# Background modulation chunks as VectorE rows, and merge adds on GpSimd, in a two-layer hybrid backbone

## The chip, the cores and the metric

The kernel is one program on one core of a Trainium2 chip. The metric is the device time of one execution in microseconds. It was 1999.94 us, the median of three runs (1998.57 to 2007.31).

## The reference

Two layers work on 256 context and 256 latent tokens of width 1024. Each layer has two sub-layers, and each is modulated by the conditioning vectors `c` (latent) and `c_ctx` (context). The modulation is six vectors ("chunks") of 1024 a layer, for both streams:

```python
mod_x = jnp.split((sc @ ada_w[l] + ada_b[l])[:, None, :], ADA_CHUNKS, axis=-1)    # sc = silu(c)
mod_c = jnp.split((scc @ ada_w[l] + ada_b[l])[None, None, :], ADA_CHUNKS, axis=-1)
hx = modulate(xx, norm1_g[l], mod_x[0], mod_x[1])          # the same for the context
mc, mx = token_mixer(hc, hx, p, lower[l], row, col, lam_init, last)
xx = xx + mod_x[2] * mx
hx = modulate(xx, norm2_g[l], mod_x[3], mod_x[4])
xx = xx + mod_x[5] * expert_choice_moe(hx, ...)
```

The token mixer has four branches (GLA scan, Hyena convolution, HGRN2 scan, differential attention). They are merged by gates and projected out:

```python
gates = jax.nn.sigmoid(gate_cols.reshape(B, L, N_BRANCH, D_MODEL))
merged = gates[:, :, 0] * (outs[0] @ w_branch[0])
for i in range(1, N_BRANCH):
    merged = merged + gates[:, :, i] * (outs[i] @ w_branch[i])
return merged @ w_out
```

Differential attention is softmax(q1 k1) - lam softmax(q2 k2) times v, per head and in blocks of 128 queries. The expert layer lets each of 16 experts take its best 32 tokens.

## The kernel before, in words

Activations are kept as columns: a tile has 128 channels on its partitions and 512 tokens along it. A scheduler sets the order of every engine's instructions when the program is built, and each engine then works off its own queue in that fixed order.

**The modulation in the first layer's mixer.** Chunks (layer, chunk) come about in two ways. `AdaBack` makes them on TensorE in the background: `Ada.step` (L465ff) loads a tile of 512 KB of `ada_w` (L469) into one of two buffers and makes four matmuls into a tile `pa`; eight such tiles are a chunk, and `mod_write` (L446) transposes the result into place. `run` (called in `load`, L842ff, with 2 credits a column block, and with half a credit at each scan level) decides when. Chunks (0,2), (0,3), (0,4) are done so: 24 tiles. `AdaRows` makes the others on VectorE, with the transposed weights `ada_t`: one tile is 128 outputs, and two instructions (L527), one for each stream, multiply it by the conditioning vector and sum along the row. The vector comes in as `cb`, spread over the partitions (L507), and goes through Silu on ScalarE (L508). Two buffers of 512 KB are loaded ahead (L515). Chunks (0,5), (1,1), (1,0) are done so: 24 tiles.

**The merges.** `merge(br, first)` (L892) goes through 8 blocks of 128 output channels. For each it loads a gate column block (L842), splits it into a high part on ScalarE (L843) and a low part on VectorE (L844), makes 24 matmuls into `pd`, takes tanh on ScalarE (L897), makes six matmuls of the branch into `pa` (its weights are split at L719, every fourth block), multiplies on VectorE (L905), and adds to the accumulator on VectorE (L911; not in the first merge). After L905, `rows.step` does one row tile in merges 0, 2 and 3 (`br != 1`): 24 blocks, 24 tiles.

**The order of the mixer.** The Hyena filters (L722 to L775) run early beside the first column blocks; then the two scans; then differential attention (from L1196), whose 32 score products are reduced on VectorE (L1250), go through exp on ScalarE (L1252), are normalised on VectorE (L1255 to L1257) and transposed on TensorE (`pm`, L428). The scheduler fills the scans and attention with merges 0 and 2. Then come hyena (L1318 to L1384), merges 3 and 1 and the out-projection (L1421), and after it the experts, whose weights come in at the full rate of the loads. GpSimd's queue also issues two loads for hyena (L1315, L1316).

Of the kernel before, what the change touches and what calls it, by code (L numbers as in the profile page):

```python
# [14 lines left out]
OP = mybir.AluOpType  # L15
# [4 lines left out]
KB = 8  # L20
# [9 lines left out]
FL = (1, 1)  # L30
DAS = (0.5, 1)
ADA = (2, 2)
ROWS = ((0, 5), (1, 1), (1, 0))
FIRST = ("gk", "gq")
AHEAD = ((0, 0), (0, 5))

# [317 lines left out]
def build(tc, ins, outT, dbg=None, stop=None):  # L354
    nc = tc.nc
    V, A, T, G, S = nc.vector, nc.scalar, nc.tensor, nc.gpsimd, nc.sync
    big = tc.tile_pool(name="big", bufs=1)
    pool = big.__enter__()
    mem = Mem(pool.tile([128, BASE], F32, name="base"), BASE, small=768)
# [140 lines left out]
    class AdaRows:  # L500


        def __init__(self, keep):
            self.todo = [(i, j) for i in range(len(ROWS)) for j in range(KB)]
            self.raw, self.junk, self.cb = [mem.take(1024, keep) for _ in range(2)], mem.take(1024, keep), mem.take(2048, keep)
            src = ins["cb"]
            S.dma_start(out=self.cb(n=2048), in_=bass.AP(tensor=src.tensor, offset=src.offset, ap=[[0, 128], [1, 2048]]))  # L507
            A.activation(self.cb(n=2048), self.cb(n=2048), AF.Silu)  # L508
            self.n = self.at = 0
            self.load(), self.load()  # L510
# [6 lines left out]

        def step(self, after):

            if self.n == len(self.todo):  # L520
                return
            i, j = self.todo[self.n]
            l, c = ROWS[i]
            b = self.raw[self.n % 2]
            with tc.issue_after(after.ins):
                for s in range(2):
                    V.tensor_tensor_reduce(self.junk() if s == 0 else b(), b(), self.cb(s * 1024, n=1024), 1.0,  # L527
                                           cs("adab", l * 48 + c * 8 + j, n=1), OP.mult, OP.add,
                                           mod[l](c * 16 + j * 2 + s, n=1))
            self.n += 1  # L530
            self.load()
            if self.n == len(self.todo):
                for b in self.raw + [self.junk, self.cb]:
                    b.free()
# [249 lines left out]
    def mixer(l, last, ada_bg, rm, sums):  # L784
# [18 lines left out]
        for k in range(KB):  # L803
# [3 lines left out]
            for s in range(2):  # L807
                c = slice(s * 256, s * 256 + 256)
# [83 lines left out]
        def merge(br, first):  # L892
            o = ob[br]
            for d in range(KB):
                p = col_block(f"m{br}{d}", t0)
                g = view(accb, d * W, W) if first and l else mem.take(W, keep_x if first else None)
                A.activation(g(), p, AF.Tanh, scale=0.5)  # L897
                if d % 4 == 0:
                    load_wb(br, d // 4)
                p = ps("s" if ada_bg.left else "a")  # L900
                for fb in range(2):
                    w = [b(((d % 4) * 2 + fb) * 128, n=128) for b in wbs]
                    mm3(p[:, 0:W], w, (o(2 * fb * W, n=W), o((2 * fb + 1) * W, n=W)),
                        fb == 0, fb == 1)
                gated = V.scalar_tensor_tensor(g(), g(), 1.0, p[:, 0:W], op0=OP.add, op1=OP.mult)  # L905
                if l == 0 and br != 1:
                    rows.step(gated)
                if first:
                    acc[d] = g
                else:  # L910
                    V.tensor_tensor(acc[d](), acc[d](), g(), op=OP.add)  # L911
                    g.free()
            o.free()

# [866 lines left out]
    for l in range(2):  # L1781
        with phase("right", F32R) as rm:
            if l == 0:
                ada = AdaBack([(0, c) for c in range(2, 5)], mem.take(2048))
            pre, ahead = mixer(l, l == 1, ada, rm, sums)
        if stop == "mixer0":
            dump("mod0", mod[0]())
# [27 lines left out]
```

## Time and profile before

| | us |
|---|---|
| median of three runs | 1999.94 (1998.57 to 2007.31) |
| the profiled execution, its own time | 2006.5 |
| its span in the profile | 2004.7 |
| TensorE (PE) busy | 1843.2 |
| VectorE (DVE) busy | 854.7 |
| ScalarE (ACT) busy | 529.9 |
| GpSimd (POOL) busy | 27.9 |

The profile is of one execution. PEld is TensorE's weight load, SP the engine that issues most loads, and SPq a queue's own part. "PEclk" or the granted clock is the share of full speed that TensorE was given: 1.00 is 2.4 GHz, 0.50 is 1.2 GHz. A name such as `pd<-r` means output and input tiles, "<-DMA base<-ada_w" the thing that ended a wait. One matmul of the program can be two records in the trace. Times on the time line are from the span's beginning.

### The profile page before, as it was taken

The page shows a single profiled execution, that of the slowest core. Times are in us where ns is not written, and L with a number is a line of the kernel's source. Part 1 is how long each engine was busy: PE and PEld are TensorE (multiplying, and loading weights), DVE is VectorE, ACT ScalarE, POOL GpSimd, SP SyncE. Part 2 cuts the span into 40 slices and gives each one's busy share as a digit, 9 for nine tenths or more (in the row PEclk, how much of TensorE's full clock was granted, in tenths as well). Part 3 has the DMA queues.
Part 4 walks back from the last instruction along what each step waited for, and adds up shares of the span by engine and source line. Part 5 has one row for each costly group of instructions (what it writes and reads, how often), then busy time and mean ns, then how long its engine had stood idle before and what let it go on. Part 6 is the DMA issues. An engine that isn't in the chain of part 4 may idle for free.

```text
span 2004.7 us, 28151 instructions
## 1 busy us (share of the span) xinstructions
PE 1843.2 (92%) x11524; PEld 1087.6 (54%) x11524; DVE 854.7 (43%) x1855; ACT 529.9 (26%) x932; POOL 27.9 (1%) x52
## 2 busy tenths in 40 slices
PE   7999999999999899999897799999998999987877
PEld 3667778877887443434232356788997333221213
DVE  5355658798743222221121345869865021110101
ACT  4433447522233110101000243447443000000000
POOL 0000000000000000000000010010000000000000
PEclk9989999999999899999999999999998999999999
DMA  8641122364545999999999855333578999999999
GB/s 312 223 140 58 64 85 78 107 236 136 194 156 218 353 399 350 387 409 409 409 409 409 302 189 180 117 106 137 200 262 336 409 409 409 409 409 409 409 409 332
DMA packets 154148, 550.07 MB, mean 274 GB/s; under 512 B 11042, under 2 KB 22690, under 8 KB 153124
## 3 DMA queue, kind: packets, MB, share of 16 engines
q1 hardware_dynamic: 153444, 545.13, 71.7%
q0 software_dynamic: 576, 3.15, 0.5%
q8 instruction: 91, 1.49, 0.3%
q14 instruction: 37, 0.30, 0.0%
HBM read 545.08 MB, written 3.15 MB: 273 GB/s over the span
## 4 chain that ended last, share of the span: by engine, by line
PE 69%; DMA 19%; DVE 7%; issue 3%; ACT 3%; SPq 0%; DVEq 0%; ACTq 0%
PE pd L431 40%; PE ps L431 15%; DMA base<-moe_w 8%; PE pm L431 7%; DMA r<-moe_w 6%; PE pa L431 4%; DMA base<-ada_w 2%; PE pm L428 1%; DMA base<-wg 1%; DVE base L527 1%; DVE r L844 1%; ACT r L843 1%; PE ps L1640 1%; DMA base<-cb 0%; DVE r L1236 0%
## 5 line engine op out<-in xcount | busy, mean ns | idle before, releaser
L431 PE MATMUL pd<-r 128*128 128x256 f32 (+3 forms) x2976 | 574.4, 364 | 12.9 <-DMA r<-moe_w 6.5
L431 PEld LDWEIGHTS pd<-r 128*128 128x128 f32 (+2 forms) x2976 | 427.3, 184 | 131.4 <-issue 53.8
L431 PE MATMUL pd<-r,r 128*128 128x512 f32 (+3 forms) x1304 | 282.6, 433 | 13.4 <-DMA r<-moe_w 10.8
L431 PEld LDWEIGHTS pd<-r,r 128*128 128x128 f32 (+2 forms) x1304 | 161.8, 166 | 105.0 <-issue 54.8
L844 DVE TENSOR_TENSOR r<-base,r 128x1024 fp32r<-128x1024 f32 x136 | 165.9, 1222 | 110.4 <-ACT r L843 110.0
L843 ACT ACTIVATE r<-base 128x1024 fp32r<-128x1024 f32 x136 | 143.4, 1058 | 252.2 <-PE pd L431 181.2
L431 PE MATMUL ps<-base 32*64 32x64 f32 (+12 forms) x2372 | 177.2, 279 | 15.1 <-DMA base<-hy 5.1
L431 PE MATMUL pd<-r,base 128*32 128x512 f32 (+1 forms) x680 | 166.5, 598 | 11.3 <-DMA r<-moe_w 10.6
L431 PEld LDWEIGHTS ps<-base 32*64 32x64 f32 (+7 forms) x2372 | 112.6, 142 | 76.3 <-issue 42.7
L431 PE MATMUL pm<-base 128*128 128x128 f32 (+12 forms) x660 | 106.1, 327 | 17.5 <-DVE base L1571 5.8
L431 PE MATMUL ps<-r,base 128*64 128x512 f32 (+4 forms) x468 | 98.6, 525 | 12.9 <-DVE base L1641 6.3
L431 PE MATMUL pd<-base 128*32 128x512 f32 (+1 forms) x408 | 100.5, 595 | 6.4 <-DMA base<-moe_w 5.6
L431 PEld LDWEIGHTS pm<-base 128*128 128x128 f32 (+5 forms) x660 | 72.8, 180 | 60.9 <-issue 33.6
L431 PEld LDWEIGHTS pd<-r,base 128*32 128x32 f32 (+1 forms) x680 | 42.0, 122 | 111.2 <-issue 76.4
L1637 DVE TENSOR_TENSOR r<-base,pd 64x512 f32<-64x512 f32 x16 | 10.9, 679 | 214.3 <-PE pd L431 214.3
L1637 DVE TENSOR_TENSOR base<-base,pd 128x512 f32<-128x512 f32 x16 | 11.0, 688 | 190.1 <-PE pd L431 155.9
L1636 ACT ACTIVATE base<-pd 128x512 f32<-128x512 f32 (+1 forms) x32 | 19.0, 594 | 251.1 <-PE pd L431 251.1
L431 PE MATMUL pa<-r,r 128*128 128x512 f32 (+1 forms) x384 | 82.4, 342 | 1.1 <-DVE base L905 1.1
L1687 ACT ACTIVATE base<-ps 32x512 f32<-32x512 f32 (+2 forms) x28 | 14.7, 525 | 251.6 <-PE ps L431 247.2
L1687 ACT ACTIVATE r<-ps 32x512 f32<-32x512 f32 (+2 forms) x32 | 15.3, 480 | 246.2 <-PE ps L431 240.3
L431 PE MATMUL pd<-base,r 128*32 128x512 f32 (+1 forms) x296 | 71.3, 597 | 9.3 <-DMA base<-moe_w 9.3
L1685 DVE COPY r<-ps 32x512 f32<-32x512 f32 (+2 forms) x32 | 17.8, 555 | 123.3 <-ACT r L1687 123.2
(246 smaller groups left out, 1728.8 us busy)
## 6 DMA issues: line engine op xcount, KB each, us to landing
r<-moe_w SPq DMA_DIRECT2D x251, 1024.0 KB, 18.1
base<-moe_w SPq DMA_DIRECT2D x131, 1024.0 KB, 17.4
base<-wg SPq DMA_DIRECT2D x152, 512.0 KB, 3.6
base<-ada_w SPq DMA_DIRECT2D x60, 512.0 KB, 4.7
base<-ada_t SPq DMA_DIRECT2D x24, 512.0 KB, 3.3
r<-ada_w SPq DMA_DIRECT2D x12, 512.0 KB, 10.2
base<-xT SPq DMA_DIRECT2D x4, 1024.0 KB, 6.8
filters<-r SPq DMA_DIRECT2D x8, 256.0 KB, 4.0
```

What stands on the lines that cost most here:

```text
L428: T.transpose(out, in_, ident)
L431: return T.matmul(out, lhsT, rhs, start=start, stop=stop, **kw)
L527: V.tensor_tensor_reduce(self.junk() if s == 0 else b(), b(), self.cb(s * 1024, n=1024), 1.0, cs("adab", l * 48 + c * 8 + j, n=1), OP.mult ...
L843: A.activation(w[0](), raw(), AF.Copy)
L844: V.tensor_tensor(w[1](), raw(), F(w[0]()), op=OP.subtract)
L1636: A.activation(s_(np_=rows), pa[0:rows, :], AF.Silu)
L1637: V.tensor_tensor(h_(np_=rows), s_(np_=rows), pb[0:rows, :], op=OP.mult)
L1640: T.transpose(p[:, q * rows:q * rows + rows], h_(q * 128, n=128, np_=rows), cs("ident", n=rows, np_=rows))
L1685: V.tensor_copy(dst, src)
L1687: A.activation(dst, src, AF.Copy)
```

## The change

Four lines do it. The row chunks become (0,4), (0,3), (0,2), (0,5), (1,1): 40 tiles in place of 24. The background on TensorE keeps one chunk, (1,0): 8 tiles in place of 24. `step` is now called in all 32 merge blocks of the first layer and does 1.25 tiles a block on the average. And the adds of merges 2 and 3 in the first layer go to GpSimd; those of merge 1 stay on VectorE. From L517 on the lines of the changed kernel are 3 higher: its row instruction is L530, its gated product L908, its add L914, its attention reduction L1253.

```diff
-ROWS = ((0, 5), (1, 1), (1, 0))
+ROWS = ((0, 4), (0, 3), (0, 2), (0, 5), (1, 1))
...
-            self.todo = [(i, j) for i in range(len(ROWS)) for j in range(KB)]
+            self.todo, self.due = [(i, j) for i in range(len(ROWS)) for j in range(KB)], 0
...
         def step(self, after):
 
-            if self.n == len(self.todo):
-                return
+            self.due += len(self.todo) / (4 * KB)
+            while self.n < self.due:
+                self.tile(after)
+
+        def tile(self, after):
             i, j = self.todo[self.n]
...
                 gated = V.scalar_tensor_tensor(g(), g(), 1.0, p[:, 0:W], op0=OP.add, op1=OP.mult)
-                if l == 0 and br != 1:
+                if l == 0:
                     rows.step(gated)
                 if first:
                     acc[d] = g
                 else:
-                    V.tensor_tensor(acc[d](), acc[d](), g(), op=OP.add)
+                    (V if l or br == 1 else G).tensor_tensor(acc[d](), acc[d](), g(), op=OP.add)
                     g.free()
...
-                ada = AdaBack([(0, c) for c in range(2, 5)], mem.take(2048))
+                ada = AdaBack([(1, 0)], mem.take(2048))
```

The scheduler's order moves with it. TensorE's queue in the filter stretch, as a difference (`pa_762` is a background chunk, `ps` the filters, `pd` a column block):

```order
 L431 MATMUL ps_604<-base 64x256
-L431 MATMUL pa_762<-base 32x256 x8
-L431 MATMUL pd_1153<-r_227,r_231 128x512 x13
-L431 MATMUL pa_762<-base 32x256 x4
-L431 MATMUL pd_1153<-r_227,r_231 128x512 x8
+L431 MATMUL pd_1122<-r_227,r_231 128x512 x24
+L431 MATMUL pd_1152<-r_227 128x512 x4
 L431 MATMUL ps_614<-r_530,base 64x256
-L431 MATMUL pa_762<-base 32x256 x4
-L431 MATMUL pd_1153<-r_227,r_231 128x512 x3
-L431 MATMUL pd_1199<-r_227 128x512
-L431 MATMUL pa_762<-base 32x256 x4
```

The background tiles that stood between the column block's matmuls are gone, and the matmuls of the next block have moved up into their place.

TensorE's queue in the second half of attention, before (`ps` from `r_678` are score products, `pm` transposes, `ps` from `base` products with v, `pd` and `pa` the merges):

```order
L431 MATMUL pd_3198<-r_227 128x512 x3
L431 MATMUL ps_2723<-base 128x64 x2
L431 MATMUL pd_3198<-r_227 128x512
L431 MATMUL pa_3224<-r_678,r_231 128x512
L431 MATMUL ps_2802<-r_678 128x512
L431 MATMUL pa_3224<-r_678,r_231 128x512 x5
L431 MATMUL pd_3238<-r_227,r_231 128x512
L431 MATMUL ps_2832<-r_678 128x256
L431 MATMUL pd_3238<-r_227,r_231 128x512 x2
L428 MATMUL pm_2787<-base 128x128 x4
L431 MATMUL pd_3238<-r_227,r_231 128x512 x3
L431 MATMUL ps_2837<-r_678 128x256
```

The same piece of attention in the changed kernel (its tile numbers are 94 lower: `ps_2708` was `ps_2802`):

```order
L431 MATMUL pd_3150<-r_227,r_231 128x512 x2
L431 MATMUL ps_2629<-base 128x64 x2
L431 MATMUL ps_2703<-r_678 128x512
L431 MATMUL pa_3096<-r_678,r_231 128x512 x5
L431 MATMUL ps_2708<-r_678 128x512
L431 MATMUL pa_3096<-r_678,r_231 128x512
L431 MATMUL ps_2738<-r_678 128x256
L428 MATMUL pm_2693<-base 128x128 x4
L431 MATMUL ps_2743<-r_678 128x256
L431 MATMUL ps_2629<-base 128x64 x4
L431 MATMUL ps_2757<-r_678 128x256
L431 MATMUL ps_2762<-r_678 128x256
```

Between these score products there were column blocks' matmuls (`pd`); now `pd` is left out but for two, and the first blocks after attention have them.

VectorE's queue at the same place before (L1250 reduces a score product, L1257 normalises):

```order
L1250 TENSOR_REDUCE base<-ps_2802 128x1
L1257 SCALAR_TENSOR_TENSOR base<-base 128x512
L1251 TENSOR_SCALAR base<-base 128x1
L1236 CAST r_678<-r_678 32x512
L1250 TENSOR_REDUCE base<-ps_2832 128x1
L844 TENSOR_TENSOR r_227<-base,r_227 128x1024
L1255 RECIPROCAL base<-base 128x2
L1251 TENSOR_SCALAR base<-base 128x1
L1250 TENSOR_REDUCE base<-ps_2837 128x1
L1256 SCALAR_TENSOR_TENSOR base<-base 128x1
L1251 TENSOR_SCALAR base<-base 128x1
L905 SCALAR_TENSOR_TENSOR base<-base,pa_3224 128x512
```

And in the changed kernel (L530 is the row instruction and its read-out):

```order
L1253 TENSOR_REDUCE base<-ps_2708 128x1
L1260 SCALAR_TENSOR_TENSOR base<-base 128x512
L1254 TENSOR_SCALAR base<-base 128x1
L1239 CAST r_678<-r_678 32x512
L1253 TENSOR_REDUCE base<-ps_2738 128x1
L530 ISA base<-base 128x1024
L530 ISA base 128x1
L1258 RECIPROCAL base<-base 128x2
L1254 TENSOR_SCALAR base<-base 128x1
L1253 TENSOR_REDUCE base<-ps_2743 128x1
L1259 SCALAR_TENSOR_TENSOR base<-base 128x1
L1254 TENSOR_SCALAR base<-base 128x1
```

The low-part split L844 and the gated product L905 have gone from between the softmax steps, and row instructions stand there. In all 16 of them stand before the last attention product L1260, five in its first half, where before all stood behind it.

## Rows read from the trace of the kernel before

**Rows 1.** The page: busy time by engine; then the chain that ended last.

```profile
PE 1843.2 (92%) x11524; PEld 1087.6 (54%) x11524; DVE 854.7 (43%) x1855; ACT 529.9 (26%) x932; POOL 27.9 (1%) x52
...
PE 69%; DMA 19%; DVE 7%; issue 3%; ACT 3%; SPq 0%; DVEq 0%; ACTq 0%
```

**Rows 2.** Stretches: us, busy us (count) of PE, PEld, DVE, ACT, POOL; PEclk, DMA share, GB/s.

```profile
400.00:450.00 50.00, 48.11 (x203) 38.81 (x202) 49.24 (x76) 12.06 (x15) 0.54 (x1) 0.97 0.68 235
...
550.00:600.00 50.00, 50.00 (x219) 40.53 (x218) 23.60 (x31) 16.93 (x23) 0.00 (x0) 1.00 0.44 155
```

**Rows 3.** TensorE: its waits for `ada_w` from 60 to 300 us; one background tile.

```profile
PE pa L431 <- DMA base<-ada_w: 4.4, 6, 1.4
...
104.03 0.64 PE L431 MATMUL pa<-base 128*32 128x256 f32 x8 [1.25 <-DMA base<-ada_w]
104.60 0.74 PE L431 MATMUL pd<-r 128*128 128x512 f32 x2
```

**Rows 4.** Chain of work from 80 to 115 us, shares by line.

```profile
by line: DMA base<-ada_w 45.9%; PE pd L431 22.5%; PE ps L431 22.5%; PE pa L431 7.5%; PE ps L428 2.4%; issue 0.5%
```

**Rows 5.** Slices of 4 us of the same stretch, columns as in rows 2.

```profile
96.00:100.00 4.00, 2.71 (x16) 1.69 (x17) 0.38 (x2) 0.42 (x1) 0.00 (x0) 1.00 0.56 186
...
104.00:108.00 4.00, 3.97 (x26) 3.37 (x27) 0.38 (x2) 1.06 (x1) 0.00 (x0) 0.73 0.71 227
108.00:112.00 4.00, 4.00 (x13) 3.22 (x12) 1.80 (x4) 0.00 (x0) 0.00 (x0) 0.50 0.01 5
```

**Rows 6.** The attention stretch, columns as in rows 2.

```profile
303.30:377.30 74.00, 73.89 (x396) 59.71 (x395) 63.24 (x179) 52.11 (x118) 0.00 (x0) 1.00 0.23 79
```

**Rows 7.** Attention stretch: TensorE's merge matmuls, VectorE's lines that the order moves.

```profile
L431 PE MATMUL pd<-r 128*128 128x512 f32 x113 | 30.5, 401 | 0.0
L431 PE MATMUL pd<-r,r 128*128 128x512 f32 x61 | 18.3, 408 | 0.0
L431 PE MATMUL pa<-r,r 128*128 128x512 f32 x42 | 12.4, 402 | 0.0
...
L1250 DVE TENSOR_REDUCE base<-ps 128x1 f32<-128x512 f32 x16 | 11.0, 687 | 3.8 <-PE ps L431 3.8
L844 DVE TENSOR_TENSOR r<-base,r 128x1024 fp32r<-128x1024 f32 x8 | 9.7, 1222 | 2.3 <-ACT r L843 2.3
```

**Rows 8.** VectorE in order of time: start us, us, engine line op.

```profile
395.91 1.28 DVE L527 CUSTOM_DVE_ANT_0 base<-base 128x1024 f32<-128x1024 f32 x1
...
397.11 0.68 DVE L905 SCALAR_TENSOR_TENSOR base<-base,pa 128x512 f32<-128x512 f32 x1
397.71 1.28 DVE L527 CUSTOM_DVE_ANT_0 base<-base 128x1024 f32<-128x1024 f32 x1
```

**Rows 9.** TensorE in a later merge block: start us, us, engine line op.

```profile
560.16 5.66 PE L431 MATMUL pd<-r 128*128 128x512 f32 x24
565.66 1.55 PE L431 MATMUL pa<-r,r 128*128 128x512 f32 x6
```

**Rows 10.** ScalarE's table load for Silu of `cb`, and VectorE's first row instruction.

```profile
390.13 1.28 ACT L508 ACT_TABLE_LOAD   x1 [1.23 <-DMA base<-cb]
...
393.37 1.29 DVE L527 CUSTOM_DVE_ANT_0 base<-base 128x1024 f32<-128x1024 f32 x1 [2.29 <-ACT base L508]
```

**Rows 11.** TensorE at hyena's beginning.

```profile
443.62 7.33 PE L431 MATMUL pd<-r 128*128 128x512 f32 x24 [1.89 <-DVE base L1328]
```

**Rows 12.** GpSimd's groups; GpSimd's casts in the second layer, and VectorE beside them.

```profile
L817 POOL TENSOR_TENSOR r<-base,r 128x256 fp32r<-128x256 f32 x3 | 2.2, 730 | 0.2
...
1349.37 3.57 POOL L1236 CAST r<-r 32x512 fp32r<-32x512 f32 x4
...
1348.87 0.41 DVE L1198 TENSOR_TENSOR base<-base 128x256 f32<-128x256 f32 x1
...
1349.94 0.83 DVE L1199 TENSOR_TENSOR base<-base 128x256 f32<-128x256 f32 x1
```

**Rows 13.** Chain in the MoE's routing: start, us, what.

```profile
650.28 1.28 ACT L1454
```

## The prediction

> **What bounds the kernel now.** Read the engines' busy time first: TensorE works 92% of the span, VectorE 43% [rows 1]. The chain of the work that ended last is TensorE's for 69% of the span, with single links of VectorE and of loads [rows 1]. Then the stretches of the first mixer: from 400 to 450 us TensorE has 48.1 of 50 us of work and VectorE 49.2, from 550 to 600 us 50.0 and 23.6 [rows 2]. So TensorE is the bound there, and VectorE in places the next one. For the change two stretches count more than these averages. In the filter stretch, 60 to 106 us, TensorE waits for the background tiles' weights [rows 3, 4]. In the attention stretch, 303 to 377 us, TensorE is busy 73.89 of 74.00 us only because merge matmuls fill the gaps of the softmax, while VectorE is busy 63.24 [rows 6].
>
> The sum is made against the profiled execution, 2006.5 us (span 2004.7). The median of the three runs is 1999.94, so I apply the difference to the median. About 0.5%, 10 us, is what a measurement can tell from no change.
>
> **Term A, what TensorE loses in work: -14.5 us.** 16 of the 24 background tiles leave TensorE; the first 8 stay and stand where they stood. One tile is 8 records, and the next matmul starts 0.57 us after it (104.03 to 104.60) [rows 3]: 16 x 0.57 = 9.1 us. TensorE waits 4.4 us for their weights in six pieces, all but one small one of which belong to tiles that go: 4.1 us [rows 3]. Where it waits, TensorE is busy 2.7 of 4 us, and the granted clock falls from 1.00 to 0.73 and then 0.50 in slices of full work: 4 x (0.27 + 0.50) = 3.1 us [rows 5]. Together 16.3. The filter branch's own matmuls then wait on their VectorE steps with less to fill in; I take 1.8 back. Bounds: -10 (the work alone) and -21.6, if the chain's links to these loads, 45.9% of its 35 us or 16.1 us [rows 4], all go and the nine tiles after 106 us add about 5.5.
>
> **Term B, attention: +24.1 us.** The 32 added VectorE instructions for sixteen tiles do not only replace TensorE's; the static order moves. Before, the copy of `cb` was issued after attention, and the first row instruction ran at 393.37 us, behind its Silu [rows 10]. In the changed order the first stands inside attention, and 16 row instructions (8 tiles) come before its last product. One takes 1.20 us with its read-out (395.91 to 397.11), a gated product 0.60 [rows 8]. VectorE's sum there: 63.2 + 16 x 1.20 (19.2), less what the order takes out: 4 low-part splits of 1.22 us that overlap their neighbour by 0.08 (4.6), 2 gated products (1.2) and one split of branch weights of the same shape as L844 (1.1) [rows 7, 8]. That is 75.5 us, against 74.
>
> TensorE's share shrinks at once. Before, 113 + 61 + 42 = 216 merge matmuls lie in the stretch [rows 7], at 0.23 us each (5.50 us for 24, from 560.16 to 565.66) [rows 9]: 49.9 us, which leaves 24.0 of 73.9 to attention itself. The changed order has 158 there: 128 up to the middle, and 30 in the second half, half of those behind the last scores. First half, to the sixteenth of 32 score products: TensorE 128 x 0.23 + 12.0 = 41.4 us, VectorE 63.2 / 2 + 5 x 1.20 = 37.6; TensorE sets it. Second half: TensorE 30 x 0.23 + 12.0 = 18.9 us, VectorE 31.6 + 11 x 1.20 - 6.9 = 37.9; VectorE sets it. So 79.3 us, of which TensorE works 60.3: it idles 19.0. I add 2 for VectorE's own waits on score matmuls (3.8 us in the stretch now, half of it [rows 7]) and 3.1 for one fall of the clock as in the filter stretch [rows 5], since TensorE would be busy only half of the second half. Bounds: 15, VectorE's bare 75.5 less 60.3; and 33, if VectorE also keeps today's idle 74.0 - 63.2 = 10.8 us [rows 6]: 19.0 + 3.1 + 10.8. Silu and its table load come between two exponentials on ScalarE: 3.24 us from 390.13 to 393.37, and 1.28 for the table back [rows 10], in the first half, where VectorE has 4 us of slack; nothing, at most +4.5 without that slack, inside the 33.
>
> **Term C, entry to hyena: -3.5 us.** After attention VectorE now works off its queue of row tiles, and TensorE waits 1.89 us for L1328 at 443.62; the next 24 matmuls take 7.33 us, against 5.66 elsewhere, at a lower clock [rows 11, 9]. 1.89 + 1.67 = 3.5. The changed order has no row instruction among hyena's steps. Bounds 0 and -5.
>
> **The small terms.** A merge block costs VectorE 1.14 + 0.28 (a quarter of a branch split) + 0.60 + 2.5 x 1.20 = 5.0 us, in merge 1 5.6 with its add, against 30 x 0.23 = 6.9 on TensorE [rows 7 to 9]: the 24 tiles of the later blocks cost nothing, and cover ends where a block's VectorE work passes 6.9. At the end of merge 1 the last block's tile, 2 x 1.20, stands ahead of the last add: +0.5 (0 to 2.4). A table load of 1.28 us in the chain at 650.28 [rows 13] is not in the changed ScalarE order: -1.3. Loads: 16 tiles of 512 KB change their source, not their size; SP's early copy of `cb` falls in a stretch with a DMA share of 0.23 [rows 6]: 0. On POOL's queue the load of the filters now stands behind one add of some 1.5 us, and hyena, which reads it, comes eight blocks later: 0.
>
> **The adds on GpSimd: 0.** Sixteen adds of 0.60 leave VectorE. On GpSimd the nearest row is a 256-wide tensor_tensor of 0.73 us [rows 12], so about 1.46 for 512. Nobody is close behind: the accumulator is next read one merge later. But it is not free for VectorE: while GpSimd runs four casts for 3.57 us, a 256-wide VectorE add takes 0.83 us beside one of 0.41 [rows 12]. If each add costs VectorE as much as it saves, nothing is won; bounds 0 and +8 (below).
> The Trainium skill, "SBUF — State Buffer", section "Who interferes with whom", speaks against this edit: VectorE instructions with two SBUF inputs, which the row instructions and splits are, and GpSimd instructions that read SBUF exclude each other for a whole instruction. The trace agrees in kind, by the doubled add; it shows no GpSimd add of this width.
>
> **Sum.** -14.5 + 24.1 - 3.5 + 0.5 - 1.3 + 0 = **+5.3 us** on 1999.94: **2005**. No change that a measurement can tell, with the sign leaning to slower.
>
> **The rivals.**
> 1. *Faster, 1989 us.* The filter branch is freed wholly and attention costs only VectorE's bare work: -21.6 + 15 - 4.3 = -10.9. For it: those links to loads are in the chain [rows 4]. Against it: TensorE itself waits only 4.4 us there [rows 3], and the first half of attention is long for TensorE, so that VectorE cannot run without a gap. 0.17.
> 2. *Slower, 2019 us.* VectorE becomes the bound of attention's second half with its present waits, at TensorE's 1.2 GHz level: -10 + 33 - 4 = +19. It decides where TensorE's idle time in attention passes 26 us, 5 more than the forecast's 21, since then the sum passes 10. For it: with 18.9 us of work in 38 TensorE would be less busy than before the fall in rows 5, and each softmax group goes from TensorE to VectorE, ScalarE and back. Against it: the row instructions themselves fill VectorE's waits. 0.27.
> 3. *Adds that block, 2014 us.* Each add holds VectorE for 1.46: a block becomes 6.5 us, 7.4 with the add's wait behind two row instructions, against 6.9; 16 x 0.5 = 8 more. It decides where VectorE in a merge block has no gap left. Against it: VectorE is busy 23.6 of 50 us in the later blocks now [rows 2]. 0.08.
> 4. *The forecast, 2005.* 0.48.
> The skill's exclusion of those two engines, named above, is rival 3's mechanism; by it VectorE would lose 1.46 us an add.
>
> **How the numbers follow.** Range 1989 to 2020: rival 1's time to just above rival 2's. Within the forecast's case the bounds of A and B put 0.1 on faster by over 0.5% and 0.27 on slower. Faster: 0.17 x 0.6 + 0.48 x 0.1 + little = 0.17. Slower: 0.27 x 0.85 + 0.48 x 0.27 + 0.08 x 0.6 = 0.41, less a little since rival 2's gaps may be filled: 0.38. Same: 0.45.
>
> **What would show it.** A: no `ada_w` wait on TensorE after about 90 us, and the attention stretch beginning near 289 us instead of 303.3 [rows 6]. B: from the first L1253 reduction to the last product about 80 us, TensorE's idle time in it near 20 us with VectorE as releaser, in the second half, and a granted clock below 0.9 there. C: no wait for hyena's VectorE step. GpSimd: 16 adds of about 1.5 us; VectorE's row instructions still 1.28. I am wrong if TensorE stays above 95% busy through attention, if the filter stretch gains under 8 us, or if the merge blocks after hyena take more than 7 us each.

## The result, and the profile after

The changed kernel takes 2023.55 us (median of 4 runs, 2021.68 to 2024.86), the kernel before 2001.47 beside it (4 runs). The ratio is **1.0101, 95% interval 1.0075 to 1.0126**: about 20 us slower. The forecast was 2005 with a range up to 2020. The time lies behind its upper end, and on the slower side, which had 0.38.

The profiled execution of the changed kernel has a span of 2022.7 us, 18.0 longer than that of before. Its page, busy time and chain of work, against [rows 1]:

```profile
PE 1849.0 (91%) x11392; PEld 1096.6 (54%) x11392; DVE 894.4 (44%) x1897; ACT 531.7 (26%) x932; POOL 61.3 (3%) x68
...
PE 69%; DMA 19%; DVE 6%; issue 3%; ACT 3%; SPq 0%; DVEq 0%; ACTq 0%
```

The shares are the same to a per cent, and the page alone doesn't say where the time went. Marks along the way do. The table has the first attention reduction, hyena's first step (L1328, or what became of it) and the out-projection's first result (L1421), all VectorE's, in the profiled executions:

| | before | changed | difference |
|---|---|---|---|
| to the first attention reduction | 303.7 | 294.6 | -9.1 |
| from there to hyena's first step | 139.0 | 165.1 | +26.1 |
| from there to the out-projection | 158.5 | 159.7 | +1.2 |
| from there to the end of the span | 1403.5 | 1403.3 | -0.2 |

So between these two executions the filter stretch gave 9.1 us, the way through attention cost 26.1, and what follows changed little: the experts' stage passes the shift on. The stretches of 50 us, columns as in rows 2:

```profile
300.00:350.00 50.00, 42.23 (x203) 33.16 (x201) 41.45 (x107) 35.02 (x69) 0.00 (x0) 0.88 0.24 85
350.00:400.00 50.00, 43.72 (x179) 33.96 (x180) 43.69 (x108) 21.26 (x47) 0.69 (x1) 0.74 0.37 126
400.00:450.00 50.00, 50.00 (x219) 40.73 (x218) 42.80 (x54) 12.31 (x16) 14.44 (x8) 1.00 0.62 211
...
550.00:600.00 50.00, 50.00 (x219) 40.72 (x218) 44.31 (x64) 12.96 (x16) 4.41 (x2) 1.00 0.58 193
```

From 400 us on TensorE is full; before, it had 48.1 of 50 us of work from 400 to 450 [rows 2]. From 300 to 400 us it is busy 86 of 100 us where it was full, and its granted clock is 0.88 and 0.74. Slices of attention show it closer (the 74 us of before were one row [rows 6]):

```profile
294.00:334.00 40.00, 38.90 (x194) 30.79 (x193) 33.41 (x91) 28.53 (x56) 0.00 (x0) 1.00 0.25 92
334.00:344.00 10.00, 6.87 (x34) 5.68 (x32) 8.18 (x22) 9.05 (x19) 0.00 (x0) 0.72 0.00 1
344.00:354.00 10.00, 6.46 (x20) 4.51 (x19) 9.28 (x30) 2.04 (x6) 0.00 (x0) 0.50 0.46 156
354.00:364.00 10.00, 7.26 (x22) 5.02 (x21) 8.47 (x23) 6.29 (x14) 0.00 (x0) 0.59 0.17 55
364.00:374.00 10.00, 7.72 (x31) 5.90 (x31) 7.88 (x25) 3.89 (x12) 0.00 (x0) 0.58 0.33 105
374.00:384.00 10.00, 8.79 (x37) 7.00 (x38) 9.44 (x21) 3.62 (x10) 0.00 (x0) 0.73 0.19 61
384.00:394.00 10.00, 9.94 (x52) 8.13 (x51) 8.31 (x21) 3.40 (x6) 0.69 (x1) 1.00 0.71 254
```

The first half is whole. From 334 us, where the order has almost no merge matmul left, TensorE is busy 6.5 to 8.8 of 10 us, and those at a granted clock of 0.50 to 0.73. Between 294 and 394 us it idles 14.1 us, and the clock takes busy time x (1 - clock) = 1.9 + 3.2 + 3.0 + 3.2 + 2.4 = 13.7 us more from 334 to 384. That is 27.8 in all, an account of TensorE's time and not of causes. Merge matmuls from the first reduction to the sixteenth score product and from there to the last product are 124 and 25 records in the trace, before 101 and 109. TensorE's longest waits from 280 to 700 us that the change brought:

```profile
PE ps L431 <- ACT base L1264: 5.5, 6, 2.3
PE pa L431 <- DVE base L908: 3.4, 1, 3.4
```

L1264 is the eviction of the transposed probabilities on ScalarE: a step of the softmax chain, which TensorE now stands and waits for. The row instructions are there as the order said, behind Silu:

```profile
311.79 1.28 ACT L508 ACT_TABLE_LOAD   x1 [2.27 <-DMA base<-cb]
313.09 1.91 ACT L508 ACTIVATE base<-base 128x2048 f32<-128x2048 f32 x1
...
315.03 1.28 DVE L530 CUSTOM_DVE_ANT_0 base<-base 128x1024 f32<-128x1024 f32 x1 [3.33 <-ACT base L508]
```

The filter stretch of the changed kernel in slices of 4 us, against [rows 5]:

```profile
100.00:104.00 4.00, 2.37 (x12) 1.99 (x11) 2.17 (x4) 2.22 (x4) 0.00 (x0) 0.86 0.38 131
104.00:108.00 4.00, 4.00 (x16) 3.51 (x16) 0.61 (x2) 0.00 (x0) 0.00 (x0) 0.50 0.00 0
...
116.00:120.00 4.00, 4.00 (x115) 3.12 (x113) 2.41 (x4) 2.95 (x8) 0.00 (x0) 0.99 0.38 137
120.00:124.00 4.00, 3.90 (x27) 3.08 (x23) 3.74 (x8) 1.21 (x2) 0.00 (x0) 0.50 0.00 0
124.00:128.00 4.00, 4.00 (x68) 3.23 (x67) 2.23 (x6) 0.62 (x1) 0.00 (x0) 0.50 0.02 6
...
136.00:140.00 4.00, 4.00 (x55) 3.78 (x57) 2.37 (x7) 0.63 (x1) 0.00 (x0) 0.50 0.24 94
140.00:144.00 4.00, 4.00 (x39) 3.78 (x35) 3.52 (x8) 0.00 (x0) 0.00 (x0) 0.52 0.02 4
```

After the first fall, which is there before as well [rows 5], the clock falls twice more: 0.50 from 120 to 128 us and 0.50 and 0.52 from 136 to 144, in slices where TensorE is full. It was full in the slice ahead of 120 too, so idle time in these slices doesn't explain the fall. The stretch from 120 to 148 us before, then changed:

```profile
120.00:148.00 28.00, 27.18 (x500) 19.77 (x497) 22.70 (x47) 9.59 (x19) 2.17 (x4) 0.94 0.35 109
```

```profile
120.00:148.00 28.00, 27.23 (x398) 23.36 (x396) 21.13 (x46) 6.64 (x12) 2.44 (x4) 0.64 0.07 21
```

The wait for `ada_w` is gone, as forecast [rows 3], and the filters' and scans' steps are what TensorE waits for:

```profile
PE ps L431 <- DVE base L987: 2.2, 4, 0.8
...
PE pa L431 <- DMA base<-ada_w: 0.3, 1, 0.3
```

Two of GpSimd's adds, then VectorE's lines of the same moment, in order of time (start us, us):

```profile
404.16 2.21 POOL L914 TENSOR_TENSOR base<-base 128x512 f32<-128x512 f32 x1 [16.61 <-DVE base L908]
...
413.02 1.28 POOL L914 TENSOR_TENSOR base<-base 128x512 f32<-128x512 f32 x1 [5.75 <-DVE base L908]
...
403.93 1.28 DVE L530 CUSTOM_DVE_ANT_0 base<-base 128x1024 f32<-128x1024 f32 x1
...
405.17 2.28 DVE L847 TENSOR_TENSOR r<-base,r 128x1024 fp32r<-128x1024 f32 x1
...
411.11 1.22 DVE L847 TENSOR_TENSOR r<-base,r 128x1024 fp32r<-128x1024 f32 x1
```

Over all 16 adds and all 80 row instructions (min/median/max in ns):

```profile
L914 POOL TENSOR_TENSOR base<-base x16: 1282/2203/2271, 404.2 to 557.3; 128x512 f32<-128x512 f32 x16
...
L530 DVE CUSTOM_DVE_ANT_0 base<-base x80: 1264/1278/2401, 315.0 to 613.7; 128x1024 f32<-128x1024 f32 x80
```

An add alone takes 1.28 us. Where it meets a row instruction that has begun, it takes 2.2, and the split that comes next on VectorE takes 2.28 in place of 1.22: by these times one waits for the other and then the other for the one. The row instruction at 403.93, which was first, keeps its 1.28; seven of the 80 take 2.2 to 2.4. The Trainium skill, "SBUF — State Buffer", section "Who interferes with whom", says that a VectorE instruction with two inputs in SBUF contends with a GpSimd instruction that reads SBUF, by an exclusive lock; the trace agrees for this pair, with these numbers. It cost little here: TensorE is full from 400 us on, and e1 below, without these adds, can't be told from the changed kernel.

### The profile page after: what moved, and what is told of

The parts are those of the page before. It is cut to its first block, busy times and chain, and to the rows that moved or that the text cites. A ratio compares the mean times of both kernels' runs of the same rounds, so it can differ in the third digit from the quotient of the medians.

```text
span 2022.7 us, 27972 instructions
## 1 busy us (share of the span) xinstructions
PE 1849.0 (91%) x11392; PEld 1096.6 (54%) x11392; DVE 894.4 (44%) x1897; ACT 531.7 (26%) x932; POOL 61.3 (3%) x68
## 4 chain that ended last, share of the span: by engine, by line
PE 69%; DMA 19%; DVE 6%; issue 3%; ACT 3%; SPq 0%; DVEq 0%; ACTq 0%
PE pd L431 40%; PE ps L431 15%; DMA base<-moe_w 9%; PE pm L431 6%; DMA r<-moe_w 6%; PE pa L431 5%; DMA base<-wg 2%; DMA base<-ada_w 1%; PE pm L428 1%; DVE r L847 1%; ACT r L846 1%; PE ps L1643 1%; DVE r L1239 0%; DMA base<-cb 0%; ACT r L1237 0%
## 5 line engine op out<-in xcount | busy, mean ns | idle before, releaser
L431 PE MATMUL pd<-r,r 128*128 128x512 f32 (+3 forms) x1304 | 280.1, 433 | 13.7 <-DMA r<-moe_w 10.9
L431 PE MATMUL ps<-base 32*64 32x64 f32 (+12 forms) x2372 | 181.7, 286 | 19.1 <-ACT base L1264 5.8
L431 PEld LDWEIGHTS ps<-base 32*64 32x64 f32 (+7 forms) x2372 | 118.3, 151 | 77.7 <-issue 38.5
L431 PE MATMUL pm<-base 128*128 128x128 f32 (+12 forms) x660 | 105.5, 325 | 17.6 <-DVE base L1574 5.8
L530 DVE CUSTOM_DVE_ANT_0 base<-base 128x1024 f32<-128x1024 f32 x80 | 108.8, 1364 | 5.7 <-ACT base L508 3.3
```

Source lines behind the costliest of these rows:

```text
L431: return T.matmul(out, lhsT, rhs, start=start, stop=stop, **kw)
```

## The experiments

All ratios are to the kernel before on the same chip in the same job. It lay between 1996 and 2020 us there, so the ratios count, not the medians. Marks as in the table above, each from one profiled execution: they tell where the time goes, the ratios how much. The part behind the out-projection, where no edit changes the code, took 1402 to 1411 us in them.

| run | row tiles: number, merges | first reduction | to hyena | to out-projection | ratio, interval |
|---|---|---|---|---|---|
| before | 24 in 0, 2, 3 | 303.7 | 139.0 | 158.5 | 1 |
| changed | 40 in all | 294.6 | 165.1 | 159.7 | 1.0101 (1.0075 to 1.0126) |
| e1 | 40 in all, adds VectorE | 295.3 | 162.4 | 159.7 | 1.0091 (1.0065 to 1.0116) |
| e2 | before, adds GpSimd | 297.5 | 143.3 | 160.3 | 1.0021 (0.9999 to 1.0042) |
| e3 | 40 in 2, 3, 1 | 295.5 | 142.8 | 170.2 | 1.0036 (1.0015 to 1.0057) |
| e5 | 24 in 2, 3, 1, two chunks out | 296.0 | 136.4 | 159.8 | 0.9969 (0.9949 to 0.9990) |
| e6 | e3, adds VectorE | 295.8 | 141.8 | 167.9 | 1.0043 (1.0027 to 1.0059) |
| e7 | 32 in 2, 3, 1 | 293.6 | 137.9 | 159.5 | 1.0014 (0.9984 to 1.0044) |
| e8 | before, 24 in 2, 3, 1 | 297.0 | 135.4 | 159.7 | 0.9994 (0.9970 to 1.0018) |
| e9 | e5 with fill | 293.2 | 135.4 | 159.7 | 0.9947 (0.9931 to 0.9963) |
| e10 | changed, buffer held | 303.6 | 143.6 | 167.6 | 1.0074 (1.0054 to 1.0095) |
| e11 | changed with fill | 294.5 | 145.2 | 173.8 | 1.0033 (1.0012 to 1.0053) |
| e12 | changed, scores thrice | 295.4 | 167.7 | 159.7 | 1.0104 (1.0068 to 1.0141) |
| e13 | e11, adds VectorE | 292.2 | 142.1 | 173.8 | 1.0025 (1.0008 to 1.0041) |
| e14 | e8, four buffers | 303.0 | 144.7 | 158.9 | 1.0046 (1.0025 to 1.0068) |
| e15 | e7, four buffers | 307.7 | 142.9 | 159.5 | 1.0047 (1.0023 to 1.0071) |
| e16 | e5, 24 in 0, 2, 3 | 293.9 | 152.8 | 158.4 | 1.0045 (1.0023 to 1.0066) |
| e18 | e7 again | 294.0 | 137.8 | 159.6 | 0.9990 (0.9964 to 1.0016) |
| e17 | e7 with fill | 299.5 | 135.5 | 160.7 | 0.9956 (0.9939 to 0.9972) |

**Are the adds the loss? e1 and e2.** The first theory after the result was that attention makes the loss; the rival was GpSimd.

```diff
-                    (V if l or br == 1 else G).tensor_tensor(acc[d](), acc[d](), g(), op=OP.add)
+                    V.tensor_tensor(acc[d](), acc[d](), g(), op=OP.add)
```

> The changed kernel with all merge adds back on VectorE. Theory (the loss is made in attention, where row instructions stand in place of merge matmuls; the adds on GpSimd are free): 2021 to 2026 us, TensorE idle about 14 us between 294 and 394 us as in the changed kernel. Rival (the 2.2 us adds on GpSimd and the VectorE instructions they double are what costs): 2012 us or less.

> The kernel before with only the adds of merges 2 and 3 moved to GpSimd. Theory (adds free): within 4 us of the kernel before, about 2001; single VectorE instructions of over 2 us beside an add, and TensorE still without a wait there. Rival (adds cost): 2010 us or more.

e1 stays at 1.0091: the rival is out for the changed kernel. e2 stands at 1.0021 and its interval touches no change. It isn't quite free: there VectorE works off its row tiles at hyena's beginning, the doubled instructions lengthen that, and TensorE's wait of 1.89 us [rows 11] becomes

```profile
PE pd L431 <- DVE base L1328: 4.8, 1, 4.8
```

**Is it row tiles inside attention? e3 and e16.** e3 takes them out of merge 0, the one that the order lays over attention:

```diff
-                if l == 0:
+                if l == 0 and br != 0:
                     rows.step(gated)
...
-            self.due += len(self.todo) / (4 * KB)
+            self.due += len(self.todo) / (3 * KB)
```

> The changed kernel with the 40 row tiles in merges 2, 3 and 1 only (1.67 a block), none in merge 0, which the order puts into attention. Theory: attention is full again (TensorE idle under 3 us and clock 1.00 from the first reduction to hyena), and what is left is the gain of the filter stretch: 1986 to 1995 us. Rival (40 tiles are too much for VectorE wherever they stand): 2010 us or more, the wait now in the later merge blocks.

The way to hyena fell from 165.1 to 142.8 us, as the theory has it, but the total only to 1.0036: the way from hyena to the out-projection rose by 10.5. Theory and rival are each half right: TensorE idles little over 1 us in attention, and the wait is now in the later merge blocks, which are too full at 1.67 tiles. TensorE's busy time there is short, and VectorE's close to 50:

```profile
500.00:550.00 50.00, 46.51 (x194) 37.01 (x193) 48.70 (x65) 12.73 (x16) 12.56 (x6) 0.97 0.62 200
550.00:600.00 50.00, 46.80 (x216) 37.51 (x214) 46.84 (x72) 15.88 (x22) 0.00 (x0) 0.99 0.70 228
```

e16 tells the place alone, at 24 tiles, with the adds on VectorE, against e5 (below). The edit is `br != 1` in place of `br != 0`.

> Run e5 with its 24 row tiles in merges 0, 2 and 3, as in the kernel before, in place of 2, 3 and 1. The order then has 10 row instructions inside attention and 166 merge matmuls beside it, against 0 and 217 in e5; tiles, adds and background are those of e5. Theory (row instructions inside attention cost what the changed kernel loses there, at any count): from the first reduction to hyena's first step 148 to 158 us against e5's 136, and 8 to 20 us slower than e5, so 1.000 to 1.007 of the kernel before. Rival (it is the 40 tiles, not their place): within 4 us of e5, 0.997.

152.8 us against 136.4, 1.0045 against 0.9969. By the traces twelve row instructions come before the last attention product, with 195 in place of 231 merge matmul records beside them (the expectation's counts, from the order, are lower); that costs some 15 us at the same number of tiles. TensorE between 300 and 350 us in e16, then in e5:

```profile
300.00:350.00 50.00, 40.81 (x201) 31.50 (x199) 41.03 (x105) 34.86 (x69) 0.00 (x0) 0.91 0.24 81
```

```profile
300.00:350.00 50.00, 49.27 (x257) 39.77 (x256) 40.18 (x108) 37.58 (x73) 0.00 (x0) 1.00 0.28 93
```

**How many tiles do the later blocks bear? e6, e7 and e18.** e6 is e3 with the adds on VectorE, e7 moves one chunk more back to TensorE:

```diff
-ROWS = ((0, 4), (0, 3), (0, 2), (0, 5), (1, 1))
+ROWS = ((0, 4), (0, 3), (0, 5), (1, 1))
...
-                ada = AdaBack([(1, 0)], mem.take(2048))
+                ada = AdaBack([(0, 2), (1, 0)], mem.take(2048))
```

> Run e3 (40 row tiles in merges 2, 3, 1) with all adds on VectorE. From hyena's first step to the out-projection's first result e3 took 170.2 us, the kernel before 158.5. If the GpSimd adds and the VectorE instructions they double made that, it is back at 158 to 161 here and the time is 1992 to 1999 us. If it is the number of row tiles (1.67 a block), it stays at 167 or more and the time near e3's.

> As e6 with one chunk more on TensorE, (0,2): 16 background tiles and 32 row tiles, 1.33 a block in merges 2, 3 and 1, adds on VectorE. Theory (VectorE has room for that many there, and the filter stretch keeps its clock with more background tiles): 158 to 161 us from hyena to the out-projection, 1993 to 1999 us in all. Rival (row tiles are dear in the later blocks at any count over one): 2003 us or more.

e6 keeps 167.9 us: it is the number, not GpSimd. e7 has 159.5, as before. Two stretches from 500 to 600 us of e6, then of e7: TensorE waits in the one, VectorE has 6 to 9 us left in the other.

```profile
500.00:550.00 50.00, 50.00 (x219) 40.65 (x218) 48.72 (x76) 13.70 (x17) 0.00 (x0) 1.00 0.65 214
550.00:600.00 50.00, 42.10 (x190) 33.41 (x189) 48.86 (x77) 14.69 (x20) 0.00 (x0) 0.92 0.75 248
```

```profile
500.00:550.00 50.00, 50.00 (x218) 40.52 (x218) 44.01 (x63) 12.78 (x16) 0.00 (x0) 1.00 0.64 209
550.00:600.00 50.00, 50.00 (x233) 40.53 (x232) 41.41 (x65) 16.29 (x22) 0.00 (x0) 1.00 0.68 229
```

The prediction's estimate of 5.0 us for a block's VectorE work at 1.25 tiles becomes 6.0 at 1.67, with its add 6.6, against 6.9 on TensorE. By it alone e6 would still be covered, and it isn't; hyena's own VectorE work, which the estimate leaves out, comes on top. e7's 159.5 us are the theory's, its time isn't: 1.0014, with an interval that spans no change. Run again (e18) it gave 0.9990 (0.9964 to 1.0016).

> Run e7 once more, with more rounds, since its interval (0.998 to 1.004) could not tell it from the kernel before. Theory (from hyena to the out-projection as before, and a shorter way from the first reduction to hyena): 0.996 to 1.000.

**What are the removed background tiles worth? e5 and e9.** e5 keeps 8 background tiles and 24 row tiles; it leaves out chunks (0,3) and (0,4), which are set to zero, and so do e9 and e16:

```diff
-ROWS = ((0, 5), (1, 1), (1, 0))
+ROWS = ((0, 2), (0, 5), (1, 1))
...
-                if l == 0 and br != 1:
+                if l == 0 and br != 0:
...
-                ada = AdaBack([(0, c) for c in range(2, 5)], mem.take(2048))
+                ada = AdaBack([(1, 0)], mem.take(2048))
+                V.memset(mod[0](48, n=32), 0.0)
```

> The kernel before with 8 background tiles on TensorE in place of 24, and 24 row tiles (one a block in merges 2, 3 and 1), adds on VectorE. Chunks (0,3) and (0,4) are set to zero and not computed. This is the gain of the removed background tiles alone. Theory (only their work goes, since the clock falls in the filter stretch with them gone): first attention reduction 8 to 10 us earlier than before (303.7), time 1989 to 1994. Rival (the prediction's 14.5 us, taken back elsewhere): reduction at 289 to 291, time 1983 to 1988.

e9 puts matmuls without loads where the tiles were:

```diff
-            S.dma_start(out=b(), in_=ins["ada_w"][self.l]...)
+            if self.l is not None:
+                S.dma_start(out=b(), in_=ins["ada_w"][self.l]...)
...
-                mm(..., b(j * 256, n=256), k == 0, k == KB - 1)
+                mm(..., b(j * 256, n=256) if self.l is not None else cs("iota", n=256), k == 0, k == KB - 1)
...
-                ada = AdaBack([(1, 0)], mem.take(2048))
+                ada = AdaBack([(1, 0), (None, 0), (None, 0)], mem.take(2048))
```

> Run e5 with 16 tiles of matmuls on resident data put where background tiles were, without loads; their results are not used, and chunks (0,3) and (0,4) are zero as in e5. Theory (without background tiles TensorE idles in the filter stretch, its clock falls to half there, and that takes back most of their work): the granted clock between 120 and 148 us is back over 0.85, the first attention reduction is at most 4 us later than in e5 (296.0) though TensorE does 9.1 us more work. Rival (the tiles cost their work): 9 us later, 304 to 306.

e5 gains 6 us, 0.9969, with its first reduction at 296.0: 7.7 us earlier, just under the theory's 8 to 10, and the rival's time is out. But e5 also moves the row tiles out of merge 0. e8 (below) does that alone, with all 24 background tiles, and reaches the out-projection at 592.1 us, e5 at 592.2; their ratios, 0.9994 and 0.9969, have intervals that overlap. So by the marks the removed tiles alone gave nothing up to there, and by the ratios no gain of theirs is shown. e9 does 9.1 us more TensorE work than e5 and its first reduction comes 2.8 us earlier, with 0.9947. The rival (the tiles cost their work) is out. That e9 is faster than e5 the ratios don't show, since the intervals overlap. The stretch from 90 to 148 us of e5, then of e9; the column behind POOL's is the granted clock:

```profile
90.00:112.00 22.00, 19.72 (x74) 14.43 (x73) 10.29 (x20) 5.93 (x8) 0.00 (x0) 0.84 0.26 91
...
120.00:148.00 28.00, 27.25 (x422) 23.38 (x417) 21.06 (x46) 6.54 (x12) 1.30 (x3) 0.63 0.08 25
```

```profile
90.00:112.00 22.00, 22.00 (x97) 13.45 (x98) 9.59 (x20) 4.85 (x9) 0.00 (x0) 1.00 0.27 92
...
120.00:148.00 28.00, 27.44 (x506) 20.89 (x506) 23.07 (x50) 9.36 (x18) 2.17 (x4) 0.98 0.12 41
```

A clock of 0.63 over 28 us of nearly full work is 10 us, more than the tiles' own work. The fill closes idle time from 90 to 112 us (19.7 to 22.0 us busy). From 120 to 148 TensorE is as busy without it as with it; there the clock is what differs, and why it falls isn't shown.

**Why did the rows come into attention? e10.** The row tiles' `cb` takes 8 KB of a partition; the background's two buffers are 8 KB. With 8 tiles in place of 24 that buffer is given back early, and in the order the load of `cb` moves forward. e10 only holds the buffer:

```diff
-                if not self.left:
-                    self.buf.free()
...
         merge(2, False)
         ada_bg.run()
+        if l == 0:
+            ada_bg.buf.free()
```

> The changed kernel with one difference: the background's 8 KB buffer is given back after merge 2 and not with the last background tile. In the order the load of cb and all row instructions then stand behind attention, with 40 tiles over the same 32 blocks and the adds on GpSimd as changed. Theory (the rows came into attention only because the background ended early and cb took its buffer, and that is the loss): TensorE idle under 3 us between the first attention reduction and the last product, about 20 us from the changed kernel gone less what the row tiles then cost at hyena's beginning: 1998 to 2008 us. Rival (the loss sits in 40 row tiles and adds anywhere): 2015 us or more.

All 40 tiles then stand behind attention in the order, and the way from the first reduction to the last product is back to 70.8 us (before 70.9, changed 87.2). So the freed buffer is what lets the rows in. But the total, 1.0074, is about 2016 us on the 2001 of the result, beside the rival's bound of 2015 and not in the theory's range: the same tiles now press on hyena and on the blocks behind it, and the filter stretch was worse in the profiled execution (first reduction 303.6; that execution took 2027.3 us, the run's median is 2021.1). TensorE is short in stretches where it was full, VectorE at 47.8 of 50:

```profile
400.00:450.00 50.00, 44.87 (x191) 35.97 (x190) 47.77 (x66) 11.94 (x15) 12.16 (x7) 0.97 0.69 230
450.00:500.00 50.00, 46.80 (x179) 32.80 (x178) 47.80 (x73) 11.20 (x15) 1.27 (x1) 0.96 0.46 148
```

**Fill in the changed kernel: e11, e13.** The edit of e9 on the changed kernel, with the adds on GpSimd (e11) and on VectorE (e13).

> The changed kernel with 16 background tiles of matmuls on resident data (no loads, results unused) behind its 8. They keep TensorE busy in the filter stretch and hold the background's buffer longer, so that the order has no row instruction in attention. Theory (clock kept, attention full): first attention reduction at 293 to 297 us though TensorE has 9.1 us more work, and 1993 to 2003 us in all. Rival (the fill costs its work): 2029 us or more, above the changed kernel.

> Run e11 with all adds on VectorE. Where row tiles stand close, at hyena's beginning, each GpSimd add lengthens a VectorE instruction from 1.28 or 1.22 to 2.2 us; run e2 put that at about 4 us. Theory: 2 to 6 us faster than e11. Rival (adds are hidden wherever they are): the same as e11 within 2 us.

Both have their first reduction at 292 to 295 us and no row in attention. 1.0033 is far from the rival's time, and a little over the theory's: from hyena to the out-projection 40 tiles behind attention cost 15 us more than before. e10 has its rows behind attention as well and no fill: 1.0074, and the two intervals just part, so here the filled kernel is the faster one. e13's 1.0025 cannot be told from e11's 1.0033, so the price of the adds stays between nothing and a few us.

**Is the clock half of the loss in attention? e12.** Each score product of the second half is issued three times.

```diff
-                        mm(p[:, 0:nk], ...)
+                        for _ in range(3 if l == 0 and pb == 1 else 1):
+                            mm(p[:, 0:nk], ...)
```

> The changed kernel with each score product of attention's second half in the first layer issued three times into the same tile: 32 more matmuls, about 7 us of work at full clock, where TensorE idles. Theory (half of the loss there is the clock, 13.7 us by the slices from 334 to 384 us, and it falls because TensorE idles): the clock in the second half rises over 0.8 and the time falls or stays, 2012 to 2024 us. Rival (VectorE's chain alone sets the stage, or the added work delays it): 2027 to 2031 us.

Undecided. The ratio is that of the changed kernel, so the added matmuls cost nothing that could be seen; but the clock rose in two of the slices only, and nothing was gained. Nor is the rise the edit's for certain: e1, with no added matmuls, has 0.80 and 0.85 in the same two slices. The slices of e12:

```profile
344.00:354.00 10.00, 6.46 (x23) 4.76 (x22) 8.82 (x28) 1.69 (x5) 0.00 (x0) 0.50 0.51 156
354.00:364.00 10.00, 8.15 (x33) 6.01 (x33) 9.36 (x26) 6.90 (x16) 0.00 (x0) 0.84 0.33 104
364.00:374.00 10.00, 9.89 (x40) 8.90 (x40) 7.63 (x23) 3.24 (x10) 0.00 (x0) 0.53 0.15 52
374.00:384.00 10.00, 8.08 (x37) 5.96 (x36) 9.33 (x21) 4.26 (x11) 0.00 (x0) 0.81 0.33 105
```

The share of the clock in attention's loss, 13.7 of 27.8 us, is therefore read from the slices and not shown by a run.

**Loads earlier: e14, e15.** Four background buffers instead of two, for e8 and e7 (`mem.take(4096)`, `range(4)`). e8 itself is the kernel before with `br != 0` in place of `br != 1`.

> The kernel before with its 24 row tiles in merges 2, 3 and 1 in place of 0, 2 and 3; nothing else. If term C is right (row tiles at hyena's beginning cost 3.5 us): 1995 to 1999 us against 2001, no wait for L1328. If not: 2001.

> Run e8 (24 background tiles, 24 row tiles in merges 2, 3, 1) with four background buffers in place of two, so that a tile's load starts two tiles earlier. Theory (the filter stretch of the kernel before loses to waits for ada_w and to the clock after them): no wait for ada_w over 1 us, clock 0.95 or more from 90 to 148 us, 0.994 to 0.998 of the kernel before. Rival (the loads come no earlier, since SP's queue holds them up): as e8, 0.999.

> Run e7 (16 background tiles, 32 row tiles in merges 2, 3, 1, adds on VectorE) with four background buffers. Theory (loads earlier, VectorE's later blocks just covered): 0.994 to 0.999 of the kernel before. Rival (32 row tiles are at the limit of the later blocks): 1.001 or more.

e8's way from the first reduction to hyena is 3.6 us shorter than before, the size of term C, and its time is not told from before's. The theories of e14 and e15 were wrong: 1.0046 and 1.0047. With four buffers the background tiles run earlier: the last starts near 98 us in e15, against 116 in e7, and near 133 in e14, against 171 in e8. Both also lose on the way to hyena (9.3 us against e8, 5.0 against e7), with a clock at half in part of attention, and that part stays open. In the filter stretch of e15 TensorE is short by 7 of 28 us, at half clock:

```profile
90.00:112.00 22.00, 20.68 (x105) 12.31 (x106) 8.25 (x16) 3.90 (x7) 0.00 (x0) 1.00 0.42 154
...
120.00:148.00 28.00, 21.04 (x393) 18.81 (x394) 20.93 (x44) 7.32 (x14) 1.91 (x4) 0.51 0.07 21
```

**A version faster than both: e17**, e7 with 8 tiles of fill, results unused.

> Run e7 (16 background tiles, 32 row tiles in merges 2, 3, 1, adds on VectorE) with 8 background tiles of matmuls on resident data behind them, results unused. Theory (fill keeps the clock of the filter stretch, and e7's row tiles are just covered): 0.994 to 0.999 of the kernel before, faster than both kernels. Rival (e7 has nothing left to gain there, and the fill costs its 4.5 us of work): 1.001 to 1.004.

0.9956 (0.9939 to 0.9972), about 9 us under the kernel before and, by the two ratios, 29 under the changed one; from e18 (0.9990) its interval doesn't part it. In the profile (filter stretch, a later stretch) the clock is 0.94, against 0.88 in e7, and TensorE is full beside 32 row tiles. But that execution was the slowest of its ten (2005.8 us), and its first reduction, 299.5, is later than e7's 293.6, so where the fill gains in this kernel isn't shown:

```profile
120.00:148.00 28.00, 27.19 (x527) 19.92 (x530) 22.45 (x47) 8.61 (x16) 2.17 (x4) 0.94 0.15 50
500.00:550.00 50.00, 50.00 (x223) 40.00 (x222) 47.57 (x71) 13.18 (x16) 0.00 (x0) 1.00 0.68 218
```

## Why the prediction was wrong, point by point

The forecast was +5.3 us, and the medians lie 22.1 apart. By the marks, as worked out below, the steps add up to +22.9. Of the 17.6 us between the two sums, 10.3 lie in Term A, 5.5 in Terms B and C together (+20.6 forecast, +26.1 measured) and 1.8 in the small terms. B and C stayed inside their bounds. Term A did not, and that carried the time out of the range: with A at its bound of -10 the steps would add up to +17.1, or 2017.

**Term A is the step that failed, by its clock.** The forecast was -14.5, with -10 and -21.6 as bounds, out of 9.1 of work, 4.1 of waits and 3.1 of clock given back. Work and waits went (the wait for `ada_w` is 0.3 us). The clock wasn't given back, it was lost: 0.64 from 120 to 148 us, against 0.94 before, which is 8 us of the 27 that TensorE is busy there in both. The sign of "3.1 given back" was wrong, and the bound of -10, "the work alone", had no room for a loss. With background tiles the clock stays up, as e9 shows (0.98), and e11 and e13 (0.96 and 1.00).

Against the profiled execution the change gained 9.1 us. That execution was itself unlucky: e2, with the same order up to the end of attention, had its first reduction at 297.5, 6.2 us earlier, and e8 at 297.0; they wait 1.5 and 3.2 us for `ada_w` in place of 4.4. Against the mean of those three, 299.4, the seven kernels with 8 background tiles, no fill and the buffer given back (293.9 to 296.0) gain 4.2. e10, which holds the buffer and has another order there, gains nothing at 303.6. That is the second fault: a sum against one execution took that execution's waits and clock for a property of the kernel.

**Term B had its place and its mechanism, and its clock was mis-sized.** The order's rows told the place: the second half of attention, with 25 merge matmul records in place of 109 and VectorE the busiest engine (43.3 of 50 us from 334 to 384). From the first reduction to the start of the last product it became 87.2 us, against 70.9 before; the forecast's stage was 79.3 against 74. TensorE lost 27.8 us, forecast 24.1. But the forecast had 21 of idle time and 3.1 of clock, and the slices have 14.1 and 13.7. The term that was mis-sized is "3.1 for one fall of the clock as in the filter stretch". The fall was priced as two slices of 4 us; TensorE was busy 65 to 88% for 50 us, and its clock was low as long. That the sum of the two came within 4 us is partly luck, since one was too large and the other too small. What the stage would take at full clock no run shows. TensorE's waits there are for ScalarE as much as for VectorE (6.7 and 6.8 us, L1264 alone 5.5), where the forecast named VectorE. Rival 2 (2019 us, "at TensorE's 1.2 GHz level") came nearest in time and had the clock; but by its own sign, idle time over 26 us, it fell: 14.1.

**Term C, -3.5,** was there: TensorE has no wait for hyena's step in the changed kernel, and e8 shows 3.6 us for such row tiles. With it attention's 27.8 make 24.3 of the 26.1 us; 1.8 are not traced. **The small terms.** From hyena to the out-projection it is +1.2 us, forecast +0.5 with nothing for the merge blocks: VectorE is at 44.3 of 50 us there and TensorE full. The table load in the experts' routing is gone, as forecast, and TensorE's wait there is 1.6 in place of 2.7 us; in the time of the rest, 0.2 us shorter, it can't be seen.

**The adds** were rightly put near zero. The single add was estimated at 1.46 us and takes 1.28 alone and 2.2 where it meets VectorE. VectorE lost 0.9 to 1.1 us at such an add, by a row instruction of 2.2 to 2.4 or a split of 2.28, and not at each of the 16. Rival 3 fell, since e1 is no faster to speak of. Rival 1 (1989) fell with term A.

By these steps: -4.2 + 26.1 + 1.2 - 0.2 = +22.9 us, against 22.1 between the medians. That they agree so well is partly luck, since most of the marks come from single executions.

## What to carry to other kernels

Background work on an engine that is the bound is not always in the way: in this filter stretch it kept TensorE's clock up, and taking it away cost about as much as it freed. Look at the granted clock in slices before and beside it, and in more than one execution. When work moves to a second engine, ask for each stretch what that engine has left there and what the static order puts out of its place; a buffer that comes free earlier can move a whole family of instructions into a stretch where they hurt. And where a stretch will be half busy, allow for a low clock over all of it, not for the one fall that the trace happens to show.

## What the runs showed of the hardware

Sixteen tiles of matmuls whose results nobody reads, 9.1 us of work, cost no time (e9 against e5: 0.9947 and 0.9969, first reduction 2.8 us earlier, clock 0.98 against 0.63 from 120 to 148 us at the same busy time). And a GpSimd add of 1.28 us and VectorE's two-input instructions hold each other up: 2.2 us for the add, 2.28 for a split of 1.22.
